# A sparse attention on TensorE: full float32 products for the values, and convolution taps held to their place in the order

## The chip, the cores and the metric

The kernel runs on one core of a Trainium2 chip. The metric is device time of one launch in microseconds (us); lower is better. Three timed runs of the kernel before gave 1773.7, 1774.44 and 1776.84 us, median 1774.44. A profiled run took 1774.05 us, of which its trace spans 1772.2 us.

## The reference, cut to what matters

The program computes two transformer blocks on 512 tokens of width 1024. The change lies in the second block, between its input projections and its output products. There a sparse attention and a depthwise convolution use the same projected input:

```
# sparse attention (selected branch and window branch): 8 heads in 2 groups, keys and values shared by a group
s = q @ k.T ;  p = softmax(masked s)          # per head, per block of 128 queries
o = gate_cmp * (p_c @ v_c) + gate_sel * (p_s @ v_s) + gate_win * (p_w @ v_w)
# convolution branch: 512 channels, 31 taps, causal
u = a * sigmoid(ag)
acc[c, t] = conv_b[c] + sum_i conv_w[i, c] * u[c, t - 30 + i]
u = silu(layer_norm(acc))
# afterwards
merged = g0 * (o @ w_nsa_out) + g1 * (u @ w_conv_out) + g2 * br_mem
```

Everything is float32, and the outputs are compared with a float32 reference.

## The kernel before, in words

**Dense products.** A product with a weight matrix is made of three fast products (`mm3`, L300 to L302): both operands are split into a high and a low half of type float32r, and high·high, high·low and low·high are added up. A weight tile of 128x2048 is loaded by DMA into `wraw`; ScalarE (ACT) writes the high half `whi` (L290) and VectorE (DVE) subtracts to get the low half `wlo` (L291). During the sparse attention a tile is split in two pieces, and GpSimd (POOL) does the second subtraction.

**The queue of dense work.** `Dense` holds a list of products. The attention code is a generator; at every `yield` the caller runs dense work of a planned cost (`dn.run(2200.0)`), and after it `convolve(1, 1)`. So TensorE (PE) gets pieces of dense work between the steps of the attention. Each engine then works off its own instructions in order.

**Sparse attention** (`sparse_attention`, L1588). It goes through 16 units: 2 groups, 4 blocks of 128 queries (from the last, with 512 keys, to the first, with 128), 2 branches. A unit takes two half steps with two heads each, and each half step has two `yield`s. In a half step

- PE makes the scores of the two heads (L1643, and L1645 for the compressed keys) into PSUM tiles `pa`;
- DVE adds the mask and takes the minimum (`sn`, `smn`, L1658), ACT makes the exponentials and their sum (L1660), DVE the reciprocal times the gate (`sden`, L1664 and L1665), and ACT scales the row (L1667);
- for the unit before, PE transposes 128 keys of the four heads (L381, `pa<-ident,sn`), ACT copies the result as high half `pt` (L235), DVE subtracts for the low half `pt` (L236), and
- in the next half step PE multiplies with the values (L1624 with the high, L1625 with the low half of `pt`). The stationary operand is `VS`, whose 128 columns hold high and low half of 64 value columns side by side. There are 40 such steps of 128 keys in all, and 8 for the compressed keys (`vcs`). `finish` (L1684) adds the two halves of the result (L1692).

**Convolution.** `ev_a` (L1734) puts 31 taps for each of the four channel blocks into two lists. Blocks 2 and 3 (62 taps) are DVE's: each tap is one instruction `oa<-upad,convw,oa` (L1750 the first, L1753 the others). Blocks 0 and 1 (62 taps) are ACT's and POOL's: ACT multiplies (L1741, L1746, into one of four buffers `ctm`) and POOL adds (L1747, 60 instructions). `convolve(n, m)` issues m taps of the second list and n of the first. A tap depends on nothing but its block's input and the tap before it, and the scheduler that fixes the order on each engine may put it ahead of instructions that come earlier in the code.

**Behind the attention** come four tiles of gate products (L1803, `ev_g1`), each with a `convolve(10, 10)` ahead of it, then all taps that are left, then the layer norm of the convolution (`conv_norm`, L1763): PE transposes `oa`, and DVE's L1767 is its first instruction.

Of the kernel before, what the change touches and what calls it, by code (L numbers as in the profile page):

```python
# [6 lines left out]
F32 = mybir.dt.float32  # L7
F32R = mybir.dt.float32r
# [3 lines left out]
AF = mybir.ActivationFunctionType  # L12
OP = mybir.AluOpType
# [3 lines left out]
S = 512  # L17
# [136 lines left out]
def body(tc, I, out):  # L154
    ctx = ExitStack()
    with ctx:
        _body(ctx, tc, I, out)


def _body(ctx, tc, I, out):  # L160
    nc = tc.nc
    pe, act, dve, pool, sync = nc.tensor, nc.scalar, nc.vector, nc.gpsimd, nc.sync


    def sub(stack, name, bufs=1, side="left", **kw):
        return stack.enter_context(tc.tile_pool(name=name, bufs=bufs, side=side, **kw))
# [6 lines left out]
    dn = Dense()  # L173
# [12 lines left out]
    def psa():  # L186
        return pa.tile([128, 512], F32, name="pa", tag="pa")
# [3 lines left out]
    def t2(name, shape=(128, 512)):  # L191
        return T2["p"].tile(list(shape), F32, name=name, tag="t2")

    def small(name, shape, bufs=4, dtype=F32):
        return tp.tile(list(shape), dtype, name=name, tag=name, bufs=bufs)

    def raw(t):
        return t.bitcast(F32)
# [19 lines left out]
    def behind(i, j):  # L218

        tc.add_manual_dep(i.ins, j.ins.name,  # L220
                          mybir.DependencyInfo(mybir.DependencyClass.NoSync, mybir.DependencyReason.DATA),
                          reason="order")
# [9 lines left out]
    def split_to(hi, lo, src, scale=None):  # L232

        if scale is None:
            act.activation(hi, src, AF.Copy)  # L235
            dve.tensor_sub(lo, src, raw(hi))  # L236
        else:
            act.activation(hi, src, AF.Copy, scale=scale)
            dve.scalar_tensor_tensor(lo, src, scale, raw(hi), op0=OP.mult, op1=OP.subtract)
# [198 lines left out]
    convw = cp.tile([128, 31, 4], F32, name="convw")  # L438
# [4 lines left out]
    def col(name, j=0):  # L443
        c = C[name] + j
        return cols[:, c:c + 1]
# [569 lines left out]
    br = rt.tile([128, 36], F32, name="br")  # L1015
# [58 lines left out]
    with ordered(nc.vector.engine, nc.scalar.engine, nc.tensor.engine):  # L1074
# [100 lines left out]
        for k in range(2):  # L1175
# [3 lines left out]
            for t in range(4):  # L1179
                pe.matmul(tab[:, 0:6 * NE], sel[:, k, t], vals[:, k, t].rearrange("p e c -> p (e c)"),  # L1180
                          start=k + t == 0, stop=k + t == 4)
        t5 = tab[:, 0:6 * NE].rearrange("p (e m c j) -> p e m c j", m=2, c=2, j=3)
        for m in range(2):
            own = slice(64 * m, 64 * m + 64)
            last = dve.tensor_reduce(cw[own], t5[own, :, m], axis=AX.X, op=OP.add)
# [28 lines left out]
    with tc.If(nr > 0):  # L1214
        with tc.tile_pool(name="rest", bufs=1, side="right") as fp:
# [14 lines left out]
            with tc.For_i(1, nr + 1) as rd:  # L1230
                with tc.For_i(0, NE) as e:
# [14 lines left out]
                    ps = psa()  # L1246
# [4 lines left out]
                    ps = psa()  # L1251
# [8 lines left out]
                    ps = psa()  # L1260
# [5 lines left out]
                    for q in range(2):  # L1266
                        ps = psa()
# [46 lines left out]
    na = sub(nas, "nsa", side="right")  # L1314
# [15 lines left out]
    kmT = kmv[:, 0:2].rearrange("p x (h n) -> p x h n", h=4)  # L1330
    vm = kmv[:, 2:4].rearrange("p x (t n) -> p x t n", t=2)
    KS = br_p.tile([128, 2, 2, 2, S], F32R, name="KS", tag="K")
    VS = na.tile([128, 2, 4, 2, 2, 64], F32R, name="VS")
    gate = na.tile([128, 4, 8, 3], F32, name="gate")
    kcT = na.tile([128, 2, 2, 32], F32R, name="kcT")
    vcs = na.tile([32, 2, 2, 64], F32R, name="vcs")
# [13 lines left out]
    def norm4(ps4, dst, a, b, w):  # L1350

        sq = t2("sq4", (128, a, b, w))
        ss, rr = small("ss4", [128, a, b], 3), small("rr4", [128, a, b], 3)
        act.activation(sq, ps4, AF.Square)
        dve.tensor_reduce(ss, sq, axis=AX.X, op=OP.add)
        rsqrt(rr, ss, [128, a, b], 1.0 / w, EPS)
        dve.tensor_mul(dst, ps4, rr[:, :, :, None].to_broadcast([128, a, b, w]))
# [116 lines left out]
    def ev_kv(br, q, ps):  # L1474
        p3 = ps.rearrange("p (t w) -> p t w", t=2)
        x = t2("kvn", (128, 2, 2, 64))
        norm4(p3[:, :, 0:128].rearrange("p t (g w) -> p t g w", g=2), x[:, :, :, 0:64], 2, 2, 64)
        kvn[br, q] = x
        v4 = p3[:, :, 128:256].rearrange("p t (g w) -> p t g w", g=2)
        split_to(VS[:, br, 2 * q:2 * q + 2, :, 0], VS[:, br, 2 * q:2 * q + 2, :, 1], v4)  # L1480

    def lay_kv(br):
        dn.flush()
# [101 lines left out]

    def sparse_attention():  # L1588
        Q = Qb["Q"]
        oT = Qb["oT"]  # L1590
        units = [(g, qt, br) for g in range(2) for qt in (3, 2, 1, 0) for br in range(2)]
        st, po, vq = {}, {}, []
# [19 lines left out]
        def cmp_turn_(g, qt, sc):  # L1612
            ps = transpose4_32(sc)
            hl = [t2("pt").bitcast(F32R)[0:32] for _ in range(2)]
            split_to(hl[0], hl[1], ps[0:32])
            vst = vcs[:, g].rearrange("p a d -> p (a d)")

            vq.append(lambda: gather_values(g, qt, vst, hl, False))

        def gather_values(g, qt, vst, hl, last):  # L1620
            first = (g, qt) not in po
            if first:
                po[g, qt] = psa()
            pe.matmul(po[g, qt], vst, hl[0], start=first, stop=False)  # L1624
            pe.matmul(po[g, qt], vst, hl[1], start=False, stop=last)  # L1625

        def transpose4_32(sc):
            ps = psa()
            for i in range(4):
                pe.transpose(ps[0:32, i * 128:i * 128 + 128], sc[:, i], ident)  # L1630
            return ps
# [18 lines left out]
        def soft(u, hf, pss):  # L1650
            g, qt, br = units[u]
            n = 128 * (qt + 1)
            if hf == 0:
                st[u] = dict(P=[], mn=small("smn", [128, 4], 4), den=small("sden", [128, 4], 4))
            d = st[u]
            for i, ps in zip((2 * hf, 2 * hf + 1), pss):
                s = t2("sn")
                dve.tensor_tensor_reduce(s[:, :n], ps[:, :n], cmask[:, 384 - 128 * qt:512], 1.0, 3.0e38,  # L1658
                                         op0=OP.add, op1=OP.min, accum_out=d["mn"][:, i:i + 1])
                act.activation(s[:, :n], s[:, :n], AF.Exp, bias=d["mn"][:, i:i + 1], scale=-1.0,  # L1660
                               accum_out=d["den"][:, i:i + 1])
                d["P"].append(s)
            ds = d["den"][:, 2 * hf:2 * hf + 2]
            dve.reciprocal(ds, ds)  # L1664
            dve.tensor_mul(ds, ds, gate[:, qt, 4 * g + 2 * hf:4 * g + 2 * hf + 2, 1 + br])  # L1665
            for i in (2 * hf, 2 * hf + 1):
                act.activation(d["P"][i][:, :n], d["P"][i][:, :n], AF.Copy, scale=d["den"][:, i:i + 1])  # L1667

        def turn(u, kt):
            g, qt, br = units[u]  # L1670
            P = st[u]["P"]
            ps = transpose4(lambda t: P[t][:, kt * 128:kt * 128 + 128])
            hl = [t2("pt").bitcast(F32R) for _ in range(2)]
            split_to(hl[0], hl[1], ps)
            vst = VS[:, br, kt, g].rearrange("p a d -> p (a d)")
            last = br == 1 and kt == qt

            def f():
                gather_values(g, qt, vst, hl, last)
                if last:  # L1680
                    dn.defer(lambda: finish(g, qt))
            vq.append(f)
# [13 lines left out]
        for u in range(nu + 1):  # L1696
            for hf in range(2):
                vals, vq[:] = list(vq), []
                if u < nu:
                    g, qt, br = units[u]  # L1700
# [30 lines left out]

    taps, ptaps = deque(), deque()

    def ev_a(j, ps):  # L1734
        if j == 0:
            Qb["up"] = r0.tile([128, 4, 30 + S], F32, name="upad", tag="U")
            pool.memset(Qb["up"][:, :, 0:30], 0.0)
        up, acc = Qb["up"], Qb["acc"][:, j]
        dve.scalar_tensor_tensor(up[:, j, 30:], tga.pop(j), 1.0, ps, op0=OP.add, op1=OP.mult)
        if j < 2:  # L1740
            ptaps.append(lambda: act.activation(acc, up[:, j, 0:S], AF.Identity, bias=col("conv_b_2", j),  # L1741
                                                scale=convw[:, 0, j:j + 1]))
            for i in range(1, 31):
                def f(i=i):
                    tm = na.tile([128, S], F32, name="ctm", tag="ctm", bufs=4)
                    act.activation(tm, up[:, j, i:i + S], AF.Copy, scale=convw[:, i, j:j + 1])  # L1746
                    pool.tensor_add(acc, acc, tm)  # L1747
                ptaps.append(f)
            return
        taps.append(lambda: dve.tensor_scalar(acc, up[:, j, 0:S], convw[:, 0, j:j + 1], col("conv_b_2", j),  # L1750
                                              op0=OP.mult, op1=OP.add))
        for i in range(1, 31):
            taps.append(lambda i=i: dve.scalar_tensor_tensor(acc, up[:, j, i:i + S], convw[:, i, j:j + 1], acc,  # L1753
                                                             op0=OP.mult, op1=OP.add))

    def convolve(n, m=2):

        for _ in range(min(m, len(ptaps))):
            ptaps.popleft()()
        for _ in range(min(n, len(taps))):  # L1760
            taps.popleft()()
# [88 lines left out]
    p3s = ExitStack()  # L1850
    T2["p"] = sub(p3s, "t2", 14)
    MODE["split"] = (2, (1,))
    for _ in sparse_attention():
        dn.run(2200.0)
        convolve(1, 1)
    dn.drain()
    p3s.close()
    nas.close()
# [26 lines left out]
        split_to(mts2["m"][0][:, j], mts2["m"][1][:, j], g)  # L1885
    lay_o()
    for c in range(4):
        dn.call(lambda: convolve(10, 10))
        dense_T(w_in2, 2840 + 1024 + 256 * c, 2, X, 8, lambda b, ps, c=c: ev_g1(2 * c + b, ps))
    dn.call(lambda: convolve(124, 124))  # L1890
    for t in range(4):
# [148 lines left out]
```

## Time and profile before

| | us |
|---|---|
| median of three timed runs | 1774.44 |
| the profiled run | 1774.05 |
| its span in the trace | 1772.2 |
| PE busy over the span | 1664.7 (94%) |
| DVE busy | 942.6 (53%) |
| ACT busy | 658.8 (37%) |
| POOL busy | 288.1 (16%) |

A busy time is the time in which at least one instruction of the engine ran. Matmuls overlap in the array, so one lasts longer than the distance from its start to the next start; the distance between starts (the pitch) is what a row of matmuls costs. In a timeline row a number in brackets is the time that the engine stood idle before it, with what released it. The 40 slices of the page are 44.3 us each; the sparse attention lies in slices 23 to 29, from 1003 to 1265 us.

### The profile page before, as it was taken

What the parts mean: (1) busy time and instruction counts of PE and PEld (TensorE: products, weight loads), DVE (VectorE), ACT (ScalarE), POOL (GpSimd) and SP (SyncE); (2) the same over time, 40 slices, a digit from 0 to 9 for tenths busy, and PEclk for the clock granted to TensorE, in tenths of its full rate; (3) what the DMA queues carried; (4) which work ended last, traced back from release to release, by engine and by line L of the source; (5) the groups of instructions that cost most, each with busy time, mean ns of one, the idle gap of its engine ahead of it and who ended that gap; (6) DMA issues with size and microseconds to landing.
All of it is one profiled execution on the core that took longest, in us unless ns stands there. A gap on an engine that the chain in (4) does not pass through costs nothing.

```text
span 1772.2 us, 24544 instructions
## 1 busy us (share of the span) xinstructions
PE 1664.7 (94%) x9766; PEld 1366.9 (77%) x9766; DVE 942.6 (53%) x2001; ACT 658.8 (37%) x1128; POOL 288.1 (16%) x276
## 2 busy tenths in 40 slices
PE   7999999999997898877799987899999999999999
PEld 7988899998787554445789876678779988888887
DVE  7642368886654210202778789954466544444221
ACT  4222245555432121212445586566433322222111
POOL 1000001100113222212100378511001111111000
PEclk9999999999999899999899988899999999999999
DMA  6223333313568899998624211122243222222240
GB/s 208 96 72 119 119 96 96 90 54 96 184 211 315 340 415 416 418 416 249 191 91 149 95 49 40 56 96 72 90 148 107 90 91 91 92 92 93 83 142 36
DMA packets 152042, 265.97 MB, mean 150 GB/s; under 512 B 11771, under 2 KB 109766, under 8 KB 147574
## 3 DMA queue, kind: packets, MB, share of 16 engines
q1 hardware_dynamic: 131542, 220.03, 34.6%
q0 software_dynamic: 13424, 35.80, 7.0%
q10 hardware_dynamic: 6960, 8.56, 1.4%
q8 instruction: 77, 1.26, 0.3%
q14 instruction: 39, 0.32, 0.1%
HBM read 248.62 MB, written 18.87 MB: 151 GB/s over the span
## 4 chain that ended last, share of the span: by engine, by line
PE 73%; DVE 12%; DMA 9%; ACT 3%; issue 2%; POOL 0%; SPq 0%; DVEq 0%; POOLq 0%; ACTq 0%
PE pd L300 18%; PE pd L302 18%; PE pd L301 18%; PE pd L888 4%; PE pa L381 3%; DVE oa L1753 3%; DMA mraw<-in_w 3%; DVE wlo L291 2%; PE pa L301 2%; PE pa L300 2%; PE pa L302 2%; DMA y_d<-yt,dest 2%; PE pd L904 2%; DMA x<-y_d 2%; DMA wlo<-in_w 1%
## 5 line engine op out<-in xcount | busy, mean ns | idle before, releaser
L291 DVE TENSOR_TENSOR wlo<-wraw,whi 128x2048 fp32r<-128x2048 f32 (+1 forms) x112 | 245.7, 2193 | 198.9 <-ACT whi L290 198.3
L290 ACT ACTIVATE whi<-wraw 128x2048 fp32r<-128x2048 f32 (+1 forms) x123 | 213.0, 1734 | 346.9 <-PE pd L301 200.7
L301 PE MATMUL pd<-wlo,hT 128*128 128x256 f32 x512 | 145.6, 284 | 1.5 <-DVE wlo L291 1.5
L300 PE MATMUL pd<-whi,hT 128*128 128x256 f32 x512 | 146.3, 286 | 0.0
L302 PE MATMUL pd<-whi,hT 128*128 128x256 f32 x512 | 145.3, 284 | 0.0
L302 PE MATMUL pd<-hnT,wlo 128*128 128x512 f32 x352 | 139.4, 396 | 0.0
L300 PE MATMUL pd<-hnT,whi 128*128 128x512 f32 x352 | 139.3, 396 | 0.0
L301 PE MATMUL pd<-hnT,whi 128*128 128x512 f32 x352 | 139.2, 395 | 0.0
L300 PE MATMUL pd<-xnT,whi 128*128 128x512 f32 (+1 forms) x280 | 114.2, 408 | 0.0
L301 PE MATMUL pd<-xnT,whi 128*128 128x512 f32 (+1 forms) x280 | 113.2, 404 | 0.0
L302 PE MATMUL pd<-xnT,wlo 128*128 128x512 f32 (+1 forms) x280 | 113.0, 403 | 0.0
L1747 POOL TENSOR_TENSOR oa<-oa,ctm 128x512 f32<-128x512 f32 x60 | 90.8, 1514 | 60.5 <-ACT ctm L1746 56.9
L301 PEld LDWEIGHTS pd<-wlo,hT 128*128 128x128 f32 x512 | 98.2, 192 | 2.0 <-DVE wlo L291 1.8
L300 PEld LDWEIGHTS pd<-whi,hT 128*128 128x128 f32 x512 | 98.2, 192 | 0.3
L302 PEld LDWEIGHTS pd<-whi,hT 128*128 128x128 f32 x512 | 98.0, 191 | 0.1
L867 DVE SCALAR_TENSOR_TENSOR sg<-sg,pd 128x256 f32<-128x256 f32 x16 | 6.7, 420 | 165.0 <-ACT sg L866 165.0
L888 PE MATMUL pd<-mraw,xs 128*64 128x256 f32 x624 | 74.9, 390 | 13.5 <-DMA mraw<-in_w 13.3
L300 PEld LDWEIGHTS pd<-hnT,whi 128*128 128x128 f32 x352 | 66.1, 188 | 16.0
L301 PEld LDWEIGHTS pd<-hnT,whi 128*128 128x128 f32 x352 | 66.1, 188 | 15.9
L302 PEld LDWEIGHTS pd<-hnT,wlo 128*128 128x128 f32 x352 | 66.1, 188 | 15.9
L300 PE MATMUL pd<-hT,whi 128*128 128x512 f32 x192 | 76.7, 399 | 0.0
L302 PE MATMUL pd<-hT,wlo 128*128 128x512 f32 x192 | 76.5, 398 | 0.0
(546 smaller groups left out, 4044.3 us busy)
## 6 DMA issues: line engine op xcount, KB each, us to landing
mraw<-in_w SPq DMA_DIRECT2D x59, 1024.0 KB
wraw<-in_w_in SPq DMA_DIRECT2D x41, 1024.0 KB
wraw<-in_w_gate SPq DMA_DIRECT2D x19, 1024.0 KB
wraw<-in_w SPq DMA_DIRECT2D x11, 1024.0 KB
wraw<-in_w_up SPq DMA_DIRECT2D x11, 1024.0 KB
wlo<-in_w SPq DMA_DIRECT2D x10, 1024.0 KB
whi<-in_w SPq DMA_DIRECT2D x10, 1024.0 KB
wraw<-in_w_down SPq DMA_DIRECT2D x10, 1024.0 KB
```

The source lines that it names most:

```text
L290: act.activation(h[:, sl], r[:, sl], AF.Copy)
L291: (pool if i in by_pool else dve).tensor_tensor(l[:, sl], r[:, sl], raw(h[:, sl]), op=OP.subtract)
L300: pe.matmul(ps, ah, bh, start=start, stop=False)
L301: pe.matmul(ps, ah, bl, start=False, stop=False)
L302: pe.matmul(ps, al, bh, start=False, stop=stop)
L381: pe.transpose(ps[:, t * 128:t * 128 + 128], src_of(t), ident)
L867: dve.scalar_tensor_tensor(sg, sg, 1.0, hid[:, 0:256], op0=OP.add, op1=OP.mult)
L888: pe.matmul(ph[64 * m:64 * m + 64, 256 * j:256 * j + 256], XS[p][:, kt, 64 * m:64 * m + 64], wt[:, m, k], start=kt == 0, stop=kt == 7)
L904: pe.matmul(py[64 * q:64 * q + 64], hs[:, k, own], wt[:, k, 512 * q:512 * q + 512], start=k == 0, stop=k == 1)
L1747: pool.tensor_add(acc, acc, tm)
L1753: taps.append(lambda i=i: dve.scalar_tensor_tensor(acc, up[:, j, i:i + S], convw[:, i, j:j + 1], acc, op0=OP.mult, op1=OP.add))
```

## The change

Two things are changed.

- **Values.** `VS` is kept as plain float32 with 64 columns, and the transposed probabilities `pt` are copied once by ACT (same number of copies, no low half by DVE). Two steps of 128 keys are held until both are there, and their float32 products are issued one behind the other, the first into output rows 0 to 63, the second into rows 64 to 127. The compressed keys keep their two products. `finish` is unchanged.
- **Taps.** Each ACT tap gets an order dependency on the last scaling instruction that was issued before it on ACT, each DVE tap on the last `sden` instruction on DVE. It adds no semaphore: the tap may only not be placed ahead of that instruction on its own engine. In the attention DVE's list is issued every second `yield` (`convolve(i % 2, 1)`), and the four calls behind it issue 9 taps each.

```diff
-    VS = na.tile([128, 2, 4, 2, 2, 64], F32R, name="VS")
+    VS = na.tile([128, 2, 4, 2, 64], F32, name="VS")
...
-        split_to(VS[:, br, 2 * q:2 * q + 2, :, 0], VS[:, br, 2 * q:2 * q + 2, :, 1], v4)
+        act.activation(VS[:, br, 2 * q:2 * q + 2], v4, AF.Copy)
...
+        odd = {}
+
+        def gather_values(g, qt, vst, pt, last):
+
+            if (g, qt) not in odd:
+                odd[g, qt] = vst, pt
+                return
             first = (g, qt) not in po
             if first:
                 po[g, qt] = psa()
-            pe.matmul(po[g, qt], vst, hl[0], start=first, stop=False)
-            pe.matmul(po[g, qt], vst, hl[1], start=False, stop=last)
+            for x, (v, p) in enumerate((odd.pop((g, qt)), (vst, pt))):
+                pe.matmul(po[g, qt][64 * x:64 * x + 64], v, p, start=first, stop=last)
...
-            dve.tensor_mul(ds, ds, gate[:, qt, 4 * g + 2 * hf:4 * g + 2 * hf + 2, 1 + br])
+            mark["dve"] = dve.tensor_mul(ds, ds, gate[:, qt, 4 * g + 2 * hf:4 * g + 2 * hf + 2, 1 + br])
             for i in (2 * hf, 2 * hf + 1):
-                act.activation(d["P"][i][:, :n], d["P"][i][:, :n], AF.Copy, scale=d["den"][:, i:i + 1])
+                mark["act"] = act.activation(d["P"][i][:, :n], d["P"][i][:, :n], AF.Copy, scale=d["den"][:, i:i + 1])
...
-            hl = [t2("pt").bitcast(F32R) for _ in range(2)]
-            split_to(hl[0], hl[1], ps)
-            vst = VS[:, br, kt, g].rearrange("p a d -> p (a d)")
+            pt = t2("pt")
+            act.activation(pt, ps, AF.Copy)
+            vst = VS[:, br, kt, g]
...
+    def paced(on, i):
+
+        if on in mark:
+            behind(i, mark[on])
+
...
-            taps.append(lambda i=i: dve.scalar_tensor_tensor(acc, up[:, j, i:i + S], convw[:, i, j:j + 1], acc,
-                                                             op0=OP.mult, op1=OP.add))
+            taps.append(lambda i=i: paced("dve", dve.scalar_tensor_tensor(acc, up[:, j, i:i + S], convw[:, i, j:j + 1],
+                                                                          acc, op0=OP.mult, op1=OP.add)))
...
-    for _ in sparse_attention():
+    for i, _ in enumerate(sparse_attention()):
         dn.run(2200.0)
-        convolve(1, 1)
+        convolve(i % 2, 1)
...
-        dn.call(lambda: convolve(10, 10))
+        dn.call(lambda: convolve(9, 10))
```

(`ev_a`'s other taps are wrapped in `paced` in the same way.)

On DVE, before, in the first group's third block of queries (taps are L1753, L236 is the low half of `pt`, L1658 the mask and minimum of the next scores):

```order
L1753 SCALAR_TENSOR_TENSOR oa<-upad,convw,oa 128x512
L1609 TENSOR_TENSOR scc<-scc,cden 128x128
L1753 SCALAR_TENSOR_TENSOR oa<-upad,convw,oa 128x512
L291 TENSOR_TENSOR wlo<-wraw,whi 128x1024
L1753 SCALAR_TENSOR_TENSOR oa<-upad,convw,oa 128x512
L236 TENSOR_TENSOR pt<-pa,pt 128x512
L1658 ISA sn,smn<-pa,cmask 128x256
L1658 ISA smn 128x1
```

The same place on DVE in the changed kernel (L1772 is the tap, L1611 what was L1609, L1672 what was L1658):

```order
L1772 SCALAR_TENSOR_TENSOR oa<-upad,convw,oa 128x512
L1609 RECIPROCAL cden<-cden 128x4
L1610 TENSOR_TENSOR cden<-cden,gate 128x4
L1611 TENSOR_TENSOR scc<-scc,cden 128x128
L291 TENSOR_TENSOR wlo<-wraw,whi 128x1024
L1672 ISA sn,smn<-pa,cmask 128x256
L1672 ISA smn 128x1
L1672 ISA sn,smn<-pa,cmask 128x256
```

Two of the three taps and the low half of `pt` have gone from between the weight split and the next minimum.

On ACT, before, one half step of the first group with 384 keys (L1746 taps, L1660 exponentials, L235 `pt`, L1667 scaling):

```order
L1746 ACTIVATE ctm<-upad,convw 128x512 x4
L1660 ACTIVATE sn,sden<-sn,smn 128x384 x2
L235 ACTIVATE pt<-pa 128x512
L1746 ACTIVATE ctm<-upad,convw 128x512
L235 ACTIVATE pt<-pa 128x512
L1667 ACTIVATE sn<-sn,sden 128x384 x2
L1746 ACTIVATE ctm<-upad,convw 128x512 x2
L290 ACTIVATE whi<-wraw 128x1024 x2
```

ACT in the changed kernel at the same unit (L1674, L1688, L1681 and L1765 are the exponentials, `pt`, scaling and taps):

```order
L1674 ACTIVATE sn,sden<-sn,smn 128x384
L1688 ACTIVATE pt<-pa 128x512
L1674 ACTIVATE sn,sden<-sn,smn 128x384
L1688 ACTIVATE pt<-pa 128x512
L1681 ACTIVATE sn<-sn,sden 128x384 x2
L1765 ACTIVATE ctm<-upad,convw 128x512 x2
L290 ACTIVATE whi<-wraw 128x1024 x2
```

Seven taps in the piece have become two, and they stand behind the scaling.

On DVE behind the attention, before (L1692 is the last `finish`, L1767 the first instruction of the layer norm):

```order
L1692 TENSOR_TENSOR oa<-pa,ot 64x2x128 x2
L236 TENSOR_TENSOR oTs<-oa,oTs 128x512 x2
L291 TENSOR_TENSOR wlo<-wraw,whi 128x2048 x3
L1767 BN_STATS bst<-pa 128x6 x2
L1768 BN_AGGR bmv<-bst 128x2
```

And in the changed kernel (L1706 the last `finish`, L1769 and L1772 taps, L1786 the first of the layer norm):

```order
L1706 TENSOR_TENSOR oa<-pa,ot 64x2x128 x2
L1772 SCALAR_TENSOR_TENSOR oa<-upad,convw,oa 128x512
L1769 TENSOR_SCALAR oa<-upad,convw,cols 128x512
L236 TENSOR_TENSOR oTs<-oa,oTs 128x512 x2
L1772 SCALAR_TENSOR_TENSOR oa<-upad,convw,oa 128x512
L291 TENSOR_TENSOR wlo<-wraw,whi 128x2048
L1772 SCALAR_TENSOR_TENSOR oa<-upad,convw,oa 128x512 x12
L291 TENSOR_TENSOR wlo<-wraw,whi 128x2048
L1772 SCALAR_TENSOR_TENSOR oa<-upad,convw,oa 128x512 x11
L291 TENSOR_TENSOR wlo<-wraw,whi 128x2048
L1772 SCALAR_TENSOR_TENSOR oa<-upad,convw,oa 128x512 x6
L1786 BN_STATS bst<-pa 128x6 x2
```

Of DVE's 62 taps 28 stand in the attention and 34 in its last step and behind it; before, the last of the 62 started at 1153.7 us, 111 us ahead of the end of the attention.

## Rows read from the trace of the kernel before

**Rows 1.** The page: PE's busy tenths and granted clock in 40 slices
```profile
PE   7999999999997898877799987899999999999999
...
PEclk9999999999999899999899988899999999999999
```

**Rows 2.** Busy by stretch; columns: length, PE, PEld, DVE, ACT, POOL, clock, DMA
```profile
1003.00:1144.00 141.00, 120.13 (x531) 95.34 (x530) 127.92 (x215) 99.25 (x199) 107.53 (x66) 0.89 0.16 53
1144.00:1265.00 121.00, 118.57 (x590) 96.15 (x589) 69.78 (x196) 77.25 (x170) 13.86 (x9) 1.00 0.22 72
1265.00:1300.00 35.00, 35.00 (x159) 28.40 (x159) 8.51 (x7) 10.50 (x10) 0.00 (x0) 1.00 0.32 107
```

**Rows 3.** Whom PE waited for, 980 to 1270 us: total, times, longest
```profile
PE pa L1643 <- DVE smn L1658: 5.2, 2, 4.4
PE pa L1625 <- DVE pt L236: 4.6, 1, 4.6
PE pa L1643 <- DVE pt L236: 3.0, 1, 3.0
```

**Rows 4.** DVE's timeline before one of these waits ends: start, duration
```profile
1101.87 2.83 DVE L1753 SCALAR_TENSOR_TENSOR oa<-upad,convw,oa 128x512 f32<-128x512 f32 x1
1104.62 0.68 DVE L236 TENSOR_TENSOR pt<-pa,pt 128x512 fp32r<-128x512 f32 x1
```

**Rows 5.** PE's timeline behind that wait; seven pitches lie between the rows
```profile
1107.22 0.63 PE L301 MATMUL pd<-omT,whi 128*128 128x512 f32 x1
...
1110.21 0.63 PE L302 MATMUL pd<-omT,wlo 128*128 128x512 f32 x1
```

**Rows 6.** PE's groups, 1003 to 1144 us, then 1144 to 1265 us
```profile
L300 PE MATMUL pd<-xnT,whi 128*128 128x512 f32 x85 | 36.4, 428 | 0.0
...
L381 PE MATMUL pa<-ident,sn 128*128 128x128 f32 x76 | 11.2, 283 | 2.6 <-DVE smn L1658 1.5 <-DVE pt L236 1.2
...
L300 PE MATMUL pd<-omT,whi 128*128 128x512 f32 x16 | 7.1, 446 | 0.0
...
L300 PE MATMUL pd<-xnT,whi 128*128 128x512 f32 x96 | 38.4, 400 | 0.0
...
L381 PE MATMUL pa<-ident,sn 128*128 128x128 f32 x84 | 12.2, 273 | 0.0
```

**Rows 7.** PE's timeline, the values' products of two steps, and what follows
```profile
1195.47 0.48 PE L1624 MATMUL pa<-pt,VS 128*128 128x512 f32 x1
1195.78 0.40 PE L1625 MATMUL pa<-pt,VS 128*128 128x512 f32 x1
...
1196.48 0.87 PE L1643 MATMUL pa<-KS,Q 128*128 128x384 f32 x4
```

**Rows 8.** PE's timeline in the first block: float32 products, 64 columns, alternating halves
```profile
601.79 3.65 PE L904 MATMUL pd<-mraw,hs 128*64 128x512 f32 x16
605.27 1.03 PE L888 MATMUL pd<-mraw,xs 128*64 128x256 f32 x8
...
674.72 1.94 PE L904 MATMUL pd<-mraw,hs 128*64 128x512 f32 x8
676.59 0.51 PE L381 MATMUL pa<-ident,sg 128*128 128x128 f32 x2
```

**Rows 9.** DVE's taps, 1003 to 1144 us, then 1144 to 1265 us
```profile
L1753 DVE SCALAR_TENSOR_TENSOR oa<-upad,convw,oa 128x512 f32<-128x512 f32 x54 | 66.7, 1245 | 0.2
...
L1753 DVE SCALAR_TENSOR_TENSOR oa<-upad,convw,oa 128x512 f32<-128x512 f32 x7 | 5.2, 740 | 0.1
```

**Rows 10.** DVE's timeline behind the attention
```profile
1277.93 2.29 DVE L291 TENSOR_TENSOR wlo<-wraw,whi 128x2048 fp32r<-128x2048 f32 x1 [8.91 <-ACT whi L290]
1289.13 2.29 DVE L291 TENSOR_TENSOR wlo<-wraw,whi 128x2048 fp32r<-128x2048 f32 x1 [8.91 <-ACT whi L290]
1299.05 1.29 DVE L1767 BATCH_NORM_STATS2 bst<-pa 128x6 f32<-128x512 f32 x2 [7.62 <-PE pa L381]
```

**Rows 11.** ACT's taps, 1003 to 1144 us
```profile
L1746 ACT ACTIVATE ctm<-upad,convw 128x512 f32<-128x512 f32 x60 | 40.1, 711 | 5.0 <-POOL oa L1747 5.0
```

**Rows 12.** Busy by stretch, 1010 to 1020 us (columns as in Rows 2)
```profile
1010.00:1020.00 10.00, 10.00 (x48) 8.10 (x47) 8.15 (x22) 7.21 (x17) 9.40 (x7) 1.00 0.34 107
```

More of the change, by code (lines that the diff above doesn't have):

```diff
@@ L1584, in memory_attention @@
                 values(i - 2, pt.pop(i - 2))
+    mark = {}
     def sparse_attention():
@@ L1616, in cmp_turn_, with f @@
             vst = vcs[:, g].rearrange("p a d -> p (a d)")
-            vq.append(lambda: gather_values(g, qt, vst, hl, False))
-        def gather_values(g, qt, vst, hl, last):
+            def f():
+                first = (g, qt) not in po
+                if first:
+                    po[g, qt] = psa()
+                for x in range(2):
+                    pe.matmul(po[g, qt], vst, hl[x], start=first and x == 0, stop=False)
+            vq.append(f)
+        odd = {}
[3 more added lines that the diff above has]
+                return
             first = (g, qt) not in po
@@ L1672, in turn @@
             ps = transpose4(lambda t: P[t][:, kt * 128:kt * 128 + 128])
-            hl = [t2("pt").bitcast(F32R) for _ in range(2)]
-            split_to(hl[0], hl[1], ps)
-            vst = VS[:, br, kt, g].rearrange("p a d -> p (a d)")
+            pt = t2("pt")
+            act.activation(pt, ps, AF.Copy)
+            vst = VS[:, br, kt, g]
             last = br == 1 and kt == qt
             def f():
-                gather_values(g, qt, vst, hl, last)
+                gather_values(g, qt, vst, pt, last)
                 if last:
@@ L1740, in ev_a @@
         if j < 2:
-            ptaps.append(lambda: act.activation(acc, up[:, j, 0:S], AF.Identity, bias=col("conv_b_2", j),
-                                                scale=convw[:, 0, j:j + 1]))
+            ptaps.append(lambda: paced("act", act.activation(acc, up[:, j, 0:S], AF.Identity, bias=col("conv_b_2", j),
+                                                             scale=convw[:, 0, j:j + 1])))
             for i in range(1, 31):
@@ L1745, in f @@
                     tm = na.tile([128, S], F32, name="ctm", tag="ctm", bufs=4)
-                    act.activation(tm, up[:, j, i:i + S], AF.Copy, scale=convw[:, i, j:j + 1])
+                    paced("act", act.activation(tm, up[:, j, i:i + S], AF.Copy, scale=convw[:, i, j:j + 1]))
                     pool.tensor_add(acc, acc, tm)
@@ L1749, in ev_a @@
             return
-        taps.append(lambda: dve.tensor_scalar(acc, up[:, j, 0:S], convw[:, 0, j:j + 1], col("conv_b_2", j),
-                                              op0=OP.mult, op1=OP.add))
+        taps.append(lambda: paced("dve", dve.tensor_scalar(acc, up[:, j, 0:S], convw[:, 0, j:j + 1], col("conv_b_2", j),
+                                                           op0=OP.mult, op1=OP.add)))
         for i in range(1, 31):
-            taps.append(lambda i=i: dve.scalar_tensor_tensor(acc, up[:, j, i:i + S], convw[:, i, j:j + 1], acc,
-                                                             op0=OP.mult, op1=OP.add))
+            taps.append(lambda i=i: paced("dve", dve.scalar_tensor_tensor(acc, up[:, j, i:i + S], convw[:, i, j:j + 1],
+                                                                          acc, op0=OP.mult, op1=OP.add)))
     def convolve(n, m=2):
```

## The prediction

> **What bounds the kernel now.** I read the page's slices first, then busy times by stretch, then PE's waits and the timelines at one of them. PE is the bound nearly everywhere: its slices show 9 or more, with a granted clock of 9 tenths [rows 1]. The sparse attention (slices 23 to 29) is one of the places where it is not: PE falls to 7 and 8 tenths there and its clock to 8.
>
> The stretches cut this in two [rows 2]. From 1003 to 1144 us, when the taps run, DVE is busy 127.9 of 141 us, POOL 107.5, ACT 99.3; PE is idle for 20.9 us and its mean granted clock is 0.89. From 1144 to 1265 us, when few taps are left, DVE is at 69.8 of 121 us, PE idle for 2.4 us, its clock 1.00. So PE waits while taps run, and hardly waits when the same attention code runs without them.
>
> PE's waits name DVE: the minimum `smn` and the low half of `pt` [rows 3]. One of them shows why. A tap took 2.83 us on DVE, the low half of `pt` stood behind it and started only at 1104.62 us [rows 4], and L1625 on PE stood idle for 4.6 us [rows 3]. Behind that wait PE ran slow: seven pitches in 2.99 us, 0.427 us each [rows 5], where 0.233 is normal (three in 0.70 us, from 1195.78 to 1196.48 [rows 7]). [...]
>
> **What the stretch would take if PE never waited.** Dense matmuls come in threes (L300 to L302), so the first stretch has 3 x (85 + 16) = 303, the second 3 x (96 + 16) = 336 (the omT count is the same in both) [rows 6]. At 0.233 us these are 70.7 and 78.4 us. PE's busy time of the second stretch less its dense work is the attention's share: 118.6 - 78.4 = 40.2 us. The first stretch did 76/84 of it by the transposes [rows 6], 36.4 us, so its PE work is 107.1 us where it took 141. To be won: 33.9 + 2.4 = 36.3 us of 262. A cross-check: idle 20.9 us plus 11% of 141 us by the clock is 36.4, with some overlap.
>
> **The change part by part.**
>
> *Low halves removed from DVE.* 40 subtractions of 0.68 us [rows 4] are 27 us off DVE and out of the chain from transposes to values. ACT's copies stay. The four subtractions for `VS` lie before the attention beside dense work on a busy PE: nothing.
>
> *Values in float32 pairs.* Two steps cost four matmuls, 1195.47 to 1196.48, 1.01 us [rows 7]. The new form is not in the attention's trace, but the first block has the same one: 128x64 stationary, 512 columns, alternate output halves, two rows of the trace per product. Sixteen rows, eight products or four pairs, take 3.48 us, 0.87 us a pair [rows 8]. Two float32 products thus share the array's time. A lone pair has more around it: a run of eight rows followed by full-width transposes takes 1.87 us [rows 8] instead of half of 3.48, so 0.13 us for leaving; I take as much for entering. A pair is then 1.13 us, 0.12 more than before, and 20 pairs cost 2.4 us. Bounds: no cost of changing gives 20 x (0.87 - 1.01) = -2.8 us; products that run one after the other, 1.74 + 0.26 us, give +19.8. I take +2.4, the nearest row being the same form.
>
> [...]
>
> *Taps on DVE.* 28 taps stay in the attention, 34 go behind it. A tap took 1.245 us beside POOL's work and 0.740 us without [rows 9]. DVE's work in the attention goes from 197.7 us [rows 2] by -71.9 (66.7 + 5.2, rows 9), -27, and 28 taps at 0.74 to 1.245 us (+21 to +35) to 120 to 134 us in some 234, 55%: lower than in the second stretch, where PE lost 2%. That leaves minima and reciprocals without a queue of taps ahead.
>
> *Taps behind the attention.* DVE idles there for 8.91 us twice and for 7.62 us before the layer norm [rows 10]. The order puts 12, 11 and 6 taps into these gaps: 8.9, 8.1 and 4.4 us at 0.740 us, POOL being idle there [rows 2]. The other five stand among the last steps. They fit, the first just so; what is late by a microsecond is a weight split needed a tile (48 matmuls, 11.2 us) later. Cost nothing; without that cover the six last taps, 4.4 us, would stand before the transposes of the layer norm. ACT's and POOL's taps end with the attention.
>
> *Taps on ACT and POOL.* Same number, about two to each half step for the whole attention, instead of 60 in the first stretch (40.1 us of ACT [rows 11]). ACT's 176.5 us of work [rows 2] fill 75% of 234 us. Behind a waiting tap stand ACT's copies of `pt` and the next exponentials, for which PE waits half a step later; the cover is the 4.4 us of planned dense work in each half step. POOL's share falls from 76% to 52%, so a tap seldom waits for a buffer.
>
> *What is late next.* I keep the second stretch's loss, 2.4 in 118.6, as the loss of the whole: 4.7 us in 228. A wait brings slow pitches too: behind 4.6 us of waiting at least 7 x 0.194 = 1.4 us [rows 5], a factor of 1.3. That makes 6.1 us.
>
> **Sum.** -36.3 + 6.1 + 2.4 = -27.8 us. Off the profiled 1774.05 us (span 1772.2 and 1.85 around it; the median of the runs is 1774.44, so both agree) that gives 1746.2 us; I say 1746.
>
> **Rivals.**
>
> *Half of it stays: ACT's taps get in the way.* Two taps, 2 x 0.67 us (40.1/60), now stand between the scaling and what follows in every half step. In the 16 half steps with 512 or 384 keys ACT is fullest; if half of these 21 us reaches PE, with the factor 1.3, 14 us are lost: 1760. For it: ACT at 75% overall. Against: the half step of dense work ahead of PE's need.
>
> *ACT becomes the bound altogether.* ACT's idle time in the second stretch, 121 - 77.25 = 43.75 us, might be blocking in order that nothing fills. Then the second half of the attention takes 77.25 + 31 x 0.67 + 43.75 = 141.8 us, the first 99.25 - 20 + 43.75 = 123: together 264.8 instead of 262, 1777. It decides once more than 42 us of a half can't be filled. Against: ACT in part waited there with no work at hand, for a dense product's end.
>
> *Slower: the loss belongs to POOL, not to DVE's queue.* DVE's taps are 0.5 us longer beside POOL [rows 9]. If every microsecond of POOL holds up DVE's short steps wherever it falls, it costs PE 33.9/107.5 = 0.315 us; POOL's 121.4 us [rows 2], now spread out, then cost 38.3 us on 228: 266.3, 4.3 more than 262, so 1778. It decides if a lightly loaded DVE still makes PE wait beside POOL. Against: from 1010 to 1020 us POOL was busy for 9.40 of 10 us and DVE for 8.15, and PE for all 10 at full clock [rows 12].
>
> [...]
>
> *The products don't pair* when only two are issued, pipelines of other matmuls before and behind: 17.4 us over the forecast, 1764. Against: rows 8.
>
> **Chances.** Forecast 63% (its own range 1738 to 1754); half of it stays 15%; products don't pair 6%; ACT the bound 5%; POOL 6%; anything else 5%, over all signs. The range, 1736 to 1765, goes from nothing lost and no cost of changing (1774 - 36.3 - 2.8 = 1735) to the unpaired products, and holds some 84%. What differs by under 0.2% (3.5 us) can't be told from no change. Faster: 63 + 15 + 6 + 3 = 87%; same: 5 + 1 = 6%; slower: 6 + 1 = 7%.
>
> **What would show it.** The attention shrinks from 262 to about 234 us, all of it in what was its first half; PE's clock is 1.00 in it; PE's waits for `smn` fall under a microsecond each and none is for a low half. A values' pair takes 1.0 to 1.2 us to the next matmul's start. DVE is at about 55%, and a layer norm starts without PE waiting for taps. I am wrong if PE's idle time in the attention stays over 12 us; then the engine that its waits name, ACT, or DVE beside a busy POOL, picks the rival.

## The result, and the profile after

The changed kernel takes 1743.05 us (median of four runs, 1742.47 to 1745.22) beside 1775.64 us for the kernel before on the same chip: a ratio of 0.9819, 95% interval 0.9807 to 0.9831. The profiled run took 1742.99 us, 31.1 us less than the profiled run before. The forecast was 1746, its range 1736 to 1765.

The page of the kernel after: PE's busy tenths and its granted clock, 40 slices of 43.5 us.

```profile
PE   7999999999999799887799999999999999999999
...
PEclk9999999999999899899899999999999999999999
```

The dip of slices 23 to 25, counted from 0 [rows 1], is gone: PE is at 9 tenths and the clock at 9 through the whole attention (slices 23 to 28 here). The windows of the kernel after, columns as in [rows 2]; the attention now ends near 1233 us:

```profile
1003.00:1144.00 141.00, 139.94 (x684) 106.13 (x682) 78.68 (x207) 107.18 (x223) 69.02 (x44) 1.00 0.21 72
1144.00:1233.00 89.00, 88.55 (x432) 65.02 (x431) 48.47 (x131) 68.40 (x147) 40.59 (x31) 1.00 0.21 67
1233.00:1268.00 35.00, 35.00 (x156) 28.29 (x155) 30.45 (x36) 10.06 (x10) 0.00 (x0) 1.00 0.31 107
```

PE idles 1.06 + 0.45 = 1.5 us in the attention where it idled 23.3 before [rows 2]. The stretch is counted from 1003 us in both (the first scores start at 1005.6 us, and 1006.0 in the kernel before); the last `finish` starts at 1231.3 us, and 1263.3 in the kernel before: 32.0 us (the second of the two instructions in each of the rows below, the kernel before first). That covers the whole gain (31.1 by the profiled runs); 0.6 us of it goes again behind the attention, where one more group of three dense products now stands. DVE is busy for 127.2 of 230 us, 55%.

```profile
1262.84 0.85 DVE L1692 TENSOR_TENSOR oa<-pa,ot 64x256 f32<-64x256 f32 x2 [1.21 <-ACT ot L1688]
```

```profile
1230.89 0.85 DVE L1706 TENSOR_TENSOR oa<-pa,ot 64x256 f32<-64x256 f32 x2
```

PE's waits in the kernel after, 980 to 1270 us (total, times, longest), which answer to [rows 3]:

```profile
PE pa L1657 <- DVE pt L236: 0.8, 1, 0.8
PE pa L381 <- ACT sn L1681: 0.3, 1, 0.3
PE pa L1659 <- DVE pt L236: 0.2, 1, 0.2
```

No wait for a minimum is left. (The low half that remains at L236 is that of the compressed keys; the prediction had expected no wait for any.) DVE's and POOL's taps of the kernel after, 1003 to 1144 us, by form (count | busy us, mean ns | idle before them):

```profile
L1766 POOL TENSOR_TENSOR oa<-oa,ctm 128x512 f32<-128x512 f32 x36 | 46.5, 1292 | 56.9 <-ACT ctm L1765 55.8
...
L1772 DVE SCALAR_TENSOR_TENSOR oa<-upad,convw,oa 128x512 f32<-128x512 f32 x15 | 11.1, 743 | 0.0
```

A DVE tap takes 743 ns although POOL still adds beside it; before it took 1245 [rows 9]. A values' pair in PE's timeline of the kernel after (start, duration):

```profile
1059.56 1.08 PE L1639 MATMUL pa<-pt,VS 128*64 128x512 f32 x4
1060.57 0.39 PE L1657 MATMUL pa<-KS,Q 128*128 128x256 f32 x1
```

From the pair's start to the next matmul's are 1.01 us, what the four matmuls took before [rows 7]. DVE's timeline behind the attention, which answers to [rows 10]:

```profile
1237.62 9.41 DVE L1772 SCALAR_TENSOR_TENSOR oa<-upad,convw,oa 128x512 f32<-128x512 f32 x12
1246.95 2.28 DVE L291 TENSOR_TENSOR wlo<-wraw,whi 128x2048 fp32r<-128x2048 f32 x1
1249.15 8.62 DVE L1772 SCALAR_TENSOR_TENSOR oa<-upad,convw,oa 128x512 f32<-128x512 f32 x11
1257.81 2.29 DVE L291 TENSOR_TENSOR wlo<-wraw,whi 128x2048 fp32r<-128x2048 f32 x1
1260.02 4.68 DVE L1772 SCALAR_TENSOR_TENSOR oa<-upad,convw,oa 128x512 f32<-128x512 f32 x6
1267.73 1.30 DVE L1786 BATCH_NORM_STATS2 bst<-pa 128x6 f32<-128x512 f32 x2 [3.02 <-PE pa L381]
```

The 12, 11 and 6 taps lie in the gaps, PE is busy for all of those 35 us, and DVE waits 3.02 us for PE ahead of the layer norm: so much cover was left.

### The profile page after: what moved, and what is told of

Its sections match the earlier page's. It is cut to its first block, busy times and chain, and to the rows that moved or that the text cites. A ratio compares the mean times of both kernels' runs of the same rounds, so it can differ in the third digit from the quotient of the medians.

```text
span 1740.9 us, 24484 instructions
## 1 busy us (share of the span) xinstructions
PE 1656.3 (95%) x9766; PEld 1347.2 (77%) x9766; DVE 893.6 (51%) x1957; ACT 657.7 (38%) x1128; POOL 276.5 (16%) x276
## 4 chain that ended last, share of the span: by engine, by line
PE 76%; DVE 9%; DMA 9%; ACT 3%; issue 2%; POOL 0%; SPq 0%; DVEq 0%; ACTq 0%; POOLq 0%
PE pd L300 19%; PE pd L302 19%; PE pd L301 19%; DMA mraw<-in_w 4%; PE pd L888 4%; PE pa L381 3%; DVE wlo L291 2%; PE pa L301 2%; PE pa L300 2%; PE pa L302 2%; DMA y_d<-yt,dest 2%; PE pd L904 2%; PE pa L1657 1%; ACT whi L290 1%; DMA wraw<-in_w 1%
## 5 line engine op out<-in xcount | busy, mean ns | idle before, releaser
L300 PE MATMUL pd<-xnT,whi 128*128 128x512 f32 (+1 forms) x280 | 112.4, 401 | 0.0
L301 PE MATMUL pd<-xnT,whi 128*128 128x512 f32 (+1 forms) x280 | 110.9, 396 | 0.0
L1766 POOL TENSOR_TENSOR oa<-oa,ctm 128x512 f32<-128x512 f32 x60 | 77.5, 1291 | 98.9 <-ACT ctm L1765 97.1
L888 PEld LDWEIGHTS pd<-mraw,xs 128*64 128x64 f32 x624 | 44.3, 141 | 42.2 <-DMA mraw<-in_w 16.6
```

The lines of the kernel that those rows point to most:

```text
L300: pe.matmul(ps, ah, bh, start=start, stop=False)
L301: pe.matmul(ps, ah, bl, start=False, stop=False)
L888: pe.matmul(ph[64 * m:64 * m + 64, 256 * j:256 * j + 256], XS[p][:, kt, 64 * m:64 * m + 64], wt[:, m, k], start=kt == 0, stop=kt == 7)
```

## The experiments

The theory on record: rows of taps on DVE keep PE waiting, and the change breaks them up. Rivals: ACT's or POOL's taps do it; the values' product does it. Medians below stand beside the 1743.05 of the changed kernel and 1773.6 to 1775.6 for the kernel before; ratios are to the kernel before on the same chip. The runs lie on several chips, and a second series of the changed kernel gave 1745.85, so a difference of 3 us between two of them says little.

**The two parts alone.** e1 has the values' part only: no tap is tied, and the lists are issued as before.

```diff
-        if on in mark:
-            behind(i, mark[on])
+        return
...
-        convolve(i % 2, 1)
+        convolve(1, 1)
```

> The new values' product alone: taps untied, both lists issued as before. DVE's queue (my theory): the 62 DVE taps still run in a burst in the first part of the attention, DVE loses only 18 low halves of 0.68 us there, 12 of 128 us, so most of the waits stay; gain of 8 to 16 us, 1759 to 1767 us. POOL's contention (rival): POOL's burst is unchanged, gain under 4 us, 1771 or more. If the product were the main cause: 1750 or less.

Measured 1780.82 us, ratio 1.0035 (1.0021 to 1.005): slower than the kernel before. The theory's range, 1759 to 1767, is missed by 14 us; the value lies in the range that the rival on POOL had named, 1771 or more. PE's largest wait in e1 (total, times, longest), then a piece of its DVE timeline and one of its POOL timeline:

```profile
PE pa L1657 <- DVE smn L1672: 15.4, 3, 6.0
```

```profile
1041.34 0.15 DVE L1678 RECIPROCAL sden<-sden 128x2 f32<-128x2 f32 x1
1041.45 1.64 DVE L1771 SCALAR_TENSOR_TENSOR oa<-upad,convw,oa 128x512 f32<-128x512 f32 x1
1043.02 1.23 DVE L1679 TENSOR_TENSOR sden<-sden,gate 128x2 f32<-128x2 f32 x1
1044.17 9.20 DVE L1771 SCALAR_TENSOR_TENSOR oa<-upad,convw,oa 128x512 f32<-128x512 f32 x6
```

```profile
1039.27 15.23 POOL L1765 TENSOR_TENSOR oa<-oa,ctm 128x512 f32<-128x512 f32 x9
```

The low halves have gone from DVE, and taps have moved up into their place: six in a row stand ahead of the minimum (L1672, which starts only at 1053.89 us), 1.53 us each, while POOL makes nine additions of 1.69 us. DVE is as busy as before (127.18 us from 1003 to 1144). The time freed on DVE was no slack: its queue refilled it. Why e1 is even slower by 7 us is open: up to the last `finish` PE idles as long as before (23.1 and 23.3 us), with its clock at 0.89 from 1003 to 1144 us in both, but five groups of three dense products fewer are done by then and stand behind it.

The rows also show what a tap is held up by: the multiply of 128x2 numbers took 1.23 us here and takes 0.16 in the kernel after (its median), while the reciprocal ahead of it, the low halves and the minima keep their durations (means from 1003 to 1144 us in e1 and in the kernel after: 158 and 163 ns, 676 and 675, 545 and 552 for a minimum of 128x384). Lengthened are instructions with two inputs in SBUF, by the same means: taps 1160 and 743 ns, gate products 710 and 428, weight splits 2210 and 1888. While POOL stood idle in e1, from 1056.81 to 1059.68 us, a tap took 0.74 us and a gate product 0.14. A tap and an addition of the row above, one by one:

```profile
1049.56 1.60 POOL L1765 TENSOR_TENSOR oa<-oa,ctm 128x512 f32<-128x512 f32 x1
1050.07 1.64 DVE L1771 SCALAR_TENSOR_TENSOR oa<-upad,convw,oa 128x512 f32<-128x512 f32 x1
```

The tap ends 0.55 us after the addition. So do all 26 lengthened taps of e1 (1.57 us or more), each after an addition; the other 34 take 0.73 to 0.83. In the kernel before, all 31 taps of over 1 us end 0.55 us after an instruction of POOL's, 28 of them after an addition and 3 after a weight split.

e2 has the taps' part only (ties, half of DVE's list behind the attention; `VS` and the low halves as before).

> The tied and moved taps alone, the values' product as before (high and low half, two matmuls a step). DVE's queue: DVE does 27 us more than in the changed kernel, about 66% busy, but without a queue of taps; 1744 to 1752 us. If both parts are needed (the low half on DVE is itself what PE waits for): 1757 to 1766 us.

Measured 1746.77 us, ratio 0.9848 (0.9832 to 0.9865): the taps' part is nearly the whole gain. Its profiled run took 1743.03 us, so it was run again beside the changed kernel:

> The changed kernel once more, beside the next one on the same chip: 1742 to 1745 us.

> The kernel with the taps' part of the change alone (ties, half behind; values as before) once more, in more rounds. If the values' product is worth what the first run said: 1745 to 1749 us, 2 to 5 us over the changed kernel. If that was scatter, as its profiled run of 1743.0 us says: within 1.5 us of the changed kernel.

Measured 1745.85 for the changed kernel (1743.05 to 1746.74) and 1746.36 for the taps' part alone (1744.25 to 1751.54). The values' part is worth 0.5 to 3.7 us by these medians, and the intervals of the two ratios (0.9811 to 0.9845, 0.9818 to 0.985) overlap: by the times alone, inconclusive below 4 us. The traces point the same way twice: from 1003 to 1242 us PE idles 5.5 us in e2 and 5.4 in e13, where it idles 1.5 in both traces of the changed kernel, and 5.0 us of e2's waits are for low halves of `pt`, where the changed kernel has 1.0. So the low halves keep PE idle for some 4 us more even when the taps are tied.

**Which ties count.** In e5 only DVE's taps are tied, in e8 only ACT's (`if on in mark and on == "dve"`, or `"act"`); the rest is the changed kernel.

> The changed kernel with only DVE's taps tied; ACT's and POOL's taps may be placed early again, so POOL runs its 60 adds in a burst. DVE's queue: PE hardly waits, 1743 to 1750 us. POOL's contention or ACT's burst (rivals): the loss of before comes back, 33.9 us per 107.5 us of POOL, 1765 to 1776 us.

> The changed kernel with only ACT's taps tied; DVE's 62 taps may be placed early again and run in a burst at the start of the attention, POOL's adds stay spread out. DVE's queue: most of the loss comes back, 1755 to 1768 us. POOL's contention or ACT's burst: 1743 to 1748 us.

e5 1753.31 us (ratio 0.9878, 0.9861 to 0.9894), e8 1759.86 (0.9917, 0.99 to 0.9933). Rows on DVE alone cost 17 us, as expected. Rows on ACT and POOL alone cost 10, between the two theories: both engines' rows count. With both untied (e1) 38 us are lost, more than 10 + 17. PE's waits in e8 (its profiled run took 1764.51 us, 4.65 over the median):

```profile
PE pa L1657 <- DVE smn L1672: 7.0, 2, 4.4
PE pa L1657 <- DVE oa L1706: 2.8, 1, 2.8
PE pa L381 <- DVE smn L1672: 2.0, 2, 1.1
```

**What in POOL's row costs.** e9 is e5 with ACT's tap cut to one column, POOL's additions whole; four standing buffers, set to zero once, take the place of the rotating `ctm` (the diff shows the tap alone).

```diff
-                    tm = na.tile([128, S], F32, name="ctm", tag="ctm", bufs=4)
-                    paced("act", act.activation(tm, up[:, j, i:i + S], AF.Copy, scale=convw[:, i, j:j + 1]))
+                    tm = Qb["ctm"][i % 4]
+                    paced("act", act.activation(tm[:, 0:1], up[:, j, i:i + 1], AF.Copy, scale=convw[:, i, j:j + 1]))
```

> Only DVE's taps are tied, ACT's and POOL's stand in a burst at the start of the attention, which by itself cost 10 us over the changed kernel. Here ACT's tap is cut to one of its 512 columns (this kernel leaves out the multiplications of the taps of blocks 0 and 1), while POOL's additions stay whole and stay in a burst. If POOL's burst is what costs those 10 us (it lengthens DVE's taps and short steps): 1750 to 1755 us, POOL over 100 us busy from 1003 to 1144. If ACT's burst is (its taps stand ahead of copies and exponentials): 1741 to 1747 us, ACT's busy time there 75 instead of 115 us.

Measured 1779.41 us (ratio 1.0038, 1.0023 to 1.0053): neither. The reason is in the waits of e9 (PE's and ACT's, 1003 to 1144 us) and in ACT's timeline there:

```profile
PE pa L1659 <- ACT pt L1688: 9.4, 1, 9.4
```

```profile
ACT ctm L1768 <- POOL oa L1769: 37.5, 34, 3.3
```

```profile
1041.19 0.29 ACT L1768 ACTIVATE ctm<-upad,convw 128x1 f32<-128x1 f32 x1 [1.95 <-POOL oa L1769]
1042.53 0.29 ACT L1768 ACTIVATE ctm<-upad,convw 128x1 f32<-128x1 f32 x1 [1.05 <-POOL oa L1769]
1043.87 0.29 ACT L1768 ACTIVATE ctm<-upad,convw 128x1 f32<-128x1 f32 x1 [1.05 <-POOL oa L1769]
...
1047.89 0.29 ACT L1768 ACTIVATE ctm<-upad,convw 128x1 f32<-128x1 f32 x1 [0.57 <-POOL oa L1769]
1048.09 1.06 ACT L1688 ACTIVATE pt<-pa 128x512 f32<-128x512 f32 x2
```

Short taps stand in longer rows, each waits for POOL to give back one of four buffers (1.34 us a piece), and `pt` stands behind them: ACT waits 37.5 us for POOL, and PE 9.4 us at once for `pt`. Here the row on the fast engine, ahead of a slow one, became a wait in the fast one's order. Cutting the tap was no clean test of POOL's share, so the next one leaves the order alone.

In e10 and e11 only POOL's addition is cut to one column; the order on PE, DVE, ACT and POOL is that of e5 (but for one spot on ACT) and that of the kernel before.

```diff
-                    pool.tensor_add(acc, acc, tm)
+                    pool.tensor_add(acc[:, 0:1], acc[:, 0:1], tm[:, 0:1])
```

> The kernel in which only DVE's taps are tied (10 us over the changed kernel), with the same order of instructions on every engine, but POOL's additions of the taps cut to one of 512 columns (this kernel leaves out most of the accumulation for blocks 0 and 1). ACT's taps stay whole and stay in rows. If those 10 us come from ACT's own tap time in front of its copies, the time stays at 1750 to 1755 us. If they come by way of POOL (ACT's taps held up by POOL for one of the four buffers, or DVE held up beside POOL): 1742 to 1747 us, and PE's 4.6 us of waits for the low half of pt go.

> The kernel before, same order of instructions on every engine, with POOL's additions of the taps cut to one of 512 columns (leaves out most of the accumulation for blocks 0 and 1). DVE's 54 taps of the first stretch should fall from 1245 to about 750 ns, 27 us less on DVE. If rows of taps by themselves make PE wait, the loss of 36 us stays for more than half: 1757 to 1772 us. If it is POOL that makes the loss, through the lengthened taps and steps on DVE and the buffers that ACT waits for, more than half of it goes: 1740 to 1756 us.

e10 1745.44 us (ratio 0.9835, 0.9816 to 0.9853): the 10 us of e5 go. e11 1741.61 us (0.9808, 0.9791 to 0.9826): the kernel before, with all its rows of taps and all its low halves, loses nothing once POOL's additions are short. The first stretch of e11, and its taps and low halves on DVE there:

```profile
1003.00:1144.00 141.00, 137.52 (x672) 110.92 (x671) 117.50 (x279) 118.95 (x241) 43.74 (x68) 1.00 0.23 75
```

```profile
L1753 DVE SCALAR_TENSOR_TENSOR oa<-upad,convw,oa 128x512 f32<-128x512 f32 x60 | 48.8, 822 | 0.3
L236 DVE TENSOR_TENSOR pt<-pa,pt 128x512 fp32r<-128x512 f32 x22 | 15.0, 683 | 1.5 <-ACT pt L235 1.4
```

DVE is busy for 117.5 of 141 us, 83%, more taps are done in the stretch than before, and PE idles only 3.5 us. So neither DVE's load, nor its low halves, nor a row of taps of 0.8 us costs PE more than those 3.5 us. What cost the 32 us is POOL's additions beside that work. Short additions take away two things at once: the hold-up of DVE, and ACT's waits for POOL to give back a buffer (5.0 us before [rows 11], 1.6 in e11). The first is the larger part: PE's waits in the kernel before name DVE for 18.2 us and ACT for 5.0, and in e8, where ACT's taps are tied and never wait for a buffer, 17 us are lost.

**How much lies behind the attention.** In e3 all ties stay, but DVE's list is issued at every `yield` (`convolve(1, 1)`); in e7 none of it in the attention (`convolve(0, 1)`).

> The changed kernel with its ties, but DVE's list of taps is issued at every yield as before, so nearly all 62 DVE taps lie in the attention and hardly one behind it. Theory (what costs is a row of taps standing together ahead of a short DVE step; a single tap of 0.75 us between two steps is covered by the dense work): the time stays at that of the changed kernel, 1741 to 1748 us, DVE busy about 66% in the attention, and each wait of PE for DVE under 2 us. Rival (DVE's total load in the attention counts, so the 34 taps behind it are what gains): 24 more taps on a loaded engine give back a third of the 36.3 us, about 1753 to 1760.

> The changed kernel, but none of DVE's taps is issued in the attention: all 62 stand behind it. Theory of the prediction (the idle time in front of the weight splits there was just enough for 12, 11 and 6 taps; 3.0 us were left before the layer norm): 28 more taps of 0.75 us are 21 us for 3 us of slack, so 14 to 18 us are lost, 1757 to 1761, and PE waits for DVE before or in the layer norm. Rival (the last wait of PE there is for something else, or dense work is brought forward into it): 1742 to 1747. If DVE's load in the attention still counted, the attention itself would be up to 1.5 us shorter.

e3 1744.53 us (ratio 0.9832, 0.9814 to 0.985): with the ties and the values' part in place, moving taps behind the attention brings nothing that these runs can tell. (The ties without either were not run.) e7 1758.37 (0.9913, 0.9897 to 0.993), 15.3 us over the changed kernel, as expected. DVE's last row of taps in e7 and its first layer norm instruction:

```profile
1259.46 14.66 DVE L1772 SCALAR_TENSOR_TENSOR oa<-upad,convw,oa 128x512 f32<-128x512 f32 x22
...
1284.07 1.30 DVE L1786 BATCH_NORM_STATS2 bst<-pa 128x6 f32<-128x512 f32 x2 [0.17 <-PE pa L381]
```

It starts 16.3 us later than at 1267.73; 28 taps of 0.74 us less the 3.02 us of cover are 17.7.

**The pairs.** In e6 both products of a pair go to the same output half, in 12 of the 20 pairs.

```diff
-                pe.matmul(po[g, qt][64 * x:64 * x + 64], v, p, start=first, stop=last)
+                h = x if n == 0 else n % 2
+                pe.matmul(po[g, qt][64 * h:64 * h + 64], v, p, start=first,
+                          stop=n == max(final[h], 0) and (n == 0 or x == 1))
```

> The changed kernel, but in the pairs of steps after the first of each result both float32 products go to the same half of the output rows (12 of the 20 pairs), so they can't share the array; the sum is the same. Theory (two products in different halves run side by side, 0.87 us the pair): 12 pairs cost 0.87 us more each, +10.4 us, about 1753.5, and such a pair takes 1.8 to 2.0 us to the next matmul's start. Rival (a float32 product of 64 columns takes half as long for another reason, and the halves play no part): 1743, pair 1.0 us.

Measured 1752.31 us (ratio 0.9879, 0.9863 to 0.9896), 9.3 us over the changed kernel, as expected. Two pairs in PE's timeline of e6, the first in two halves, the second in one:

```profile
1029.70 1.08 PE L1642 MATMUL pa<-pt,VS 128*64 128x512 f32 x4
1030.71 0.62 PE L1661 MATMUL pa<-KS,Q 128*128 128x384 f32 x2
...
1034.22 1.93 PE L1642 MATMUL pa<-pt,VS 128*64 128x512 f32 x4
1036.08 0.50 PE L300 MATMUL pd<-xnT,whi 128*128 128x512 f32 x1
```

1.01 us against 1.86: products in different halves run side by side. Twelve times 0.85 us are 10.2.

## Why the prediction was right, and where it was not

*The bound and what could be won.* Right: all of the gain is in the attention. Its work without waits was put at 262 - 36.3 = 225.7 us, and with 1.5 us of idle time left it now takes 230 (1003 to 1233); by the last `finish` it is 32.0 us shorter. Of the difference of 4.3 us between 36.3 and 32.0, 1.5 are idle time; the other 2.8 lie in PE's work itself, and no run took them apart.

*The loss that stays.* Mis-sized: 6.1 us forecast, 1.5 measured as idle time, with a granted clock of 1.00.

*Values in pairs.* Mis-sized by a little: +2.4 us forecast, 0 measured per pair (1.01 us and 1.01). That they share the array was right (1.01 us a pair in two halves, 1.86 in one), and e6 gives its price when they don't: 0.85 us a pair, where I had 0.87. The 0.13 us around a lone pair, which I counted twice, shows at most once: 1.01 is 0.87 + 0.14.

With 1.5 and 0 us in place of 6.1 and 2.4, and the 2.8 us added, the sum is -32.0 instead of -27.8: what the last `finish` shows (-31.1 by the profiled runs, -32.6 by the medians).

*Taps behind the attention.* Right as to cost (nothing, with 3.02 us of cover), and e7 confirms the price beyond the cover. As to what it brings: nothing that the runs can tell (e3).

*Low halves removed.* Right about DVE's 27 us, wrong in what I let them mean: removed alone they save PE no idle time (e1), and in its order taps fill the gap.

*The step that failed* is the cause: "That leaves minima and reciprocals without a queue of taps ahead", with DVE's load as the measure. e11 has the queue, and a load of 83% where the step relied on 55%, and no loss. What costs is DVE's taps and short steps beside POOL's additions: they hold each other up, so a queue of six taps takes 9.2 us instead of 4.4. Neither queue alone is the cause: with only DVE's broken up 10 us stay lost (e5), with only POOL's broken up 17 (e8). The number came out all the same because the change breaks up both; as far as the cause goes, that was luck. By the cause as I stated it, tying DVE's taps alone would have been enough, and e5 shows that it isn't. I had this in hand as the rival "the loss belongs to POOL" and gave it 6%. Its first half was right: POOL holds up DVE, and taking POOL's work away takes the whole loss away. Its second half was wrong: that each microsecond of POOL costs PE the same wherever it falls. Spread out, POOL's 109.6 us in the attention cost PE 1.5 us at most. My argument against it, that PE ran on from 1010 to 1020 us with POOL busy [rows 12], only showed that ten such microseconds had cover. What spoke for it, and stood in the trace before, is the duration of one short instruction; e11 decided it. DVE's groups of the kernel before, 1003 to 1144 us, the multiply with the gate and the reciprocal ahead of it:

```profile
L1665 DVE TENSOR_TENSOR sden<-sden,gate 128x2 f32<-128x2 f32 x14 | 10.1, 720 | 0.1
...
L1664 DVE RECIPROCAL sden<-sden 128x2 f32<-128x2 f32 x15 | 2.3, 151 | 3.2 <-ACT sn L1660 3.2
```

Both work on 128x2 numbers; the one with two inputs in SBUF takes five times as long (720 and 151 ns). Why DVE and POOL hold each other up, no run shows.

*ACT's taps.* The forecast was right to put their cost at nothing while they are tied two to a half step: ACT is busy 175.6 of 230 us (76%; 75% forecast), and PE waits 0.3 us for it. e9 shows the rival's mechanism in another form, ACT held up through the four buffers (37.5 us).

What stays open: in e5, how the 10 us split between DVE held up by POOL and ACT waiting for buffers (6.4 us in that stretch). More buffers there were not tried. Open too is why e1 is slower than the kernel before. None of the complete variants beats the changed kernel; e3 is level with it.

## What to carry to other kernels

Look at the durations of short instructions as well as at the load: here a 128x2 multiply of 0.7 us instead of 0.16 showed that the engine was held up, and a row of filler work cost far more there than its length alone says (six taps 9.2 us instead of 4.4). Filler work that depends on nothing was best tied to a step on its own engine, and on both engines at once (one alone left 10 or 17 us); freeing time on the busy engine without that let more filler move up. To find which of two engines that hold each other up is the cause, shorten one engine's instructions and leave the order as it is, and check what else they released.

## What the runs showed of the hardware

DVE's instructions with two inputs in SBUF and POOL's additions held each other up: in the row of e1, taps took 1.53 us on average (0.74 in the kernel after) and additions 1.69 (1.29 in the kernel after), and each lengthened tap ended 0.55 us after an addition. There a tap and an addition together took 1.7 us, less than 0.74 + 1.29, so a part of each still overlapped. In the kernel after no tap was lengthened (60 taps, 0.73 to 0.75 us), but the multiply of 128x2 numbers was in 12 of 32 cases (0.52 to 1.60 us; 0.15 to 0.16 in the others), 11 times right ahead of a tap. Here, in the timeline of all engines, it lasts until POOL's weight split ends (1059.94 + 2.94 = 1062.88), and the tap behind it takes its usual time:

```profile
1059.94 2.94 POOL L291 TENSOR_TENSOR wlo<-wraw,whi 128x1024 fp32r<-128x1024 f32 x1 [2.11 <-ACT whi L290]
...
1061.29 1.60 DVE L1679 TENSOR_TENSOR sden<-sden,gate 128x2 f32<-128x2 f32 x1
1062.81 0.74 DVE L1772 SCALAR_TENSOR_TENSOR oa<-upad,convw,oa 128x512 f32<-128x512 f32 x1
```
